# Strassen pairs in three of the down projection's four chunks, another cut of its last chunk, and regrouped recurrence matmuls

## The chip, the cores and the metric

One core of a Trainium2 chip runs the whole program. The metric is the device time of one execution in microseconds (us), the median of three. Lower is better.

## The reference, cut to what matters

One layer of a hybrid decoder for a prompt of 1024 rows and for 8 sample rows of one token each, width 1024. h2 has 1024 channels, the inner layer of the feed-forward part 4096.

```python
h = _rmsnorm(x, p['norm_mix']) * (1 + sc1) + sh1
proj = h @ p['w_in']
...
o_hg, S_new = _hgrn2_recurrence(qh, kh, vh, lh, S_hg.astype(f32))
...
y, h_new = _ssd_recurrence(...)
...
u = jax.nn.sigmoid(ga + bma) * (o_hg @ p['w_br_a']) + jax.nn.sigmoid(gb + bmb) * (y @ p['w_br_b'])
x = x + g1 * (u @ p['w_out'])

h2 = _rmsnorm(x, p['norm_mlp']) * (1 + sc2) + sh2
x = x + g2 * (jnp.square(jax.nn.relu(h2 @ p['w_up'])) @ p['w_down'])
...
y_prompt = _rmsnorm(xp, norm_final)
y_sample = _rmsnorm(xs, norm_final)
```

All of it is float32. The two recurrences run over the 1024 rows in chunks; the HGRN2 one has 8 heads, the SSM one 8 groups of 4 heads. The outputs are y, the new states of both recurrences and the last rows before the convolution.

## The kernel before

Activations lie with channels on the partitions: a *plane* is 128 channels by NT = 1032 columns (1024 prompt rows, 8 samples). Every float32 plane and weight is kept as two halves of the type that TensorE takes in one pass, hi (the value rounded) and lo (the rest), and a product is three matmuls: wh with lo, wl with hi, wh with hi.

A **dense block** makes one output plane from eight input planes: `load_w` (L47) brings a weight of 128 x 1024 by a DMA of SP into a staging tile "wr" (three buffers), ACT makes `wh` (L54), VectorE `wl` (L56), each with two buffers. `dense_split` (L79) runs over one of three column splits of SW = 344: 8 planes x 3 matmuls into a PSUM tile `acc` (three buffers), 72 for the whole block, and then an eviction. `tick` (L95) is called after every three matmuls: a recurrence can run beside the dense blocks as a generator, and each `yield n` lets n matmuls of dense blocks go by before it goes on. So the rows of HGRN heads (`hgrn_recurrence`, L460) and SSM groups (`ssm_recurrence`, L783) lie between the dense matmuls: in HGRN `kv_ps` (L529) and `o_ps` (L547), each in two half groups of four chunks, and the row sums of `row_rstd` (L559, matmul L564); in SSM, for each pair of heads, `kvx_ps` (L846), then `y_ps` (L881, from w and xdt, 64 output rows) and `yi_ps` (L885, from cv and hs), each in two halves.

A **Strassen pair** (`strassen_pair`, L1277) makes two output planes at once by seven products instead of eight, in the order 1, 7, 6, 2, 5, 4, 3; each product is two column quarters of HQ = 258 with 4 planes x 3 matmuls (L1304). Products 1, 2 and 3 take quarters of the planes as they are, 7, 6, 5 and 4 differences of them, the tiles `th` and `tl`. `differences` (L1104, lines L1108 on VectorE) makes four differences of 516 columns from two planes. `strassen_weights` (L1236) combines and splits the two weights (L1250).

`phase_ffn` (L1320) ends the kernel. The up projection is 2 + 4 dense blocks, 12 pairs and 2 dense blocks; its 32 output planes go to memory (`ad`, L1331). The down projection adds up four chunks of eight such planes, `down[c * 8 + m]` being the weight for output plane m. In chunks 0 to 2 each of eight dense blocks ends in `gated_add` (L1020, L1024, and L1027 and L1028 for the samples' 8 columns), which adds to x1. With block m goes `act` for plane m of the next chunk: `load_split_in` (L914) loads it by SP into the later `lo` (L920), ACT makes hi (L921) and VectorE lo (L922). Planes have two sets of buffers ("A1" and "Q3", "A0" and "Q2"), which chunks take in turn. The last chunk goes over the splits in the order LAST = (2, 0, 1); within one, over eight blocks, whose weights are loaded anew in each; after each block `sum_sq` (L1037, L1038) adds a square to `sqa`, and at the end `rstd_model` (L1041, matmul `ss` L1044, then the root, L169 to L174) and eight scalings (L1391) with eight DMAs of y (L1392).

A scheduler sets each engine's order from the order of the program and from priorities (`high_priority` for loads, splits and evictions); each engine, and SP's queue of loads, then goes in order.

## Time and profile before

| | us |
|---|---|
| three timed runs, median | 2486.53 (2486.45 to 2491.19) |
| the profiled execution | 2488.51 |
| its span | 2486.7 |
| TensorE busy | 2447.1 |
| VectorE busy | 1607.8 |
| ScalarE (ACT) busy | 1087.9 |
| dense 344-column matmuls on the chain, share | 58% |
| Strassen matmuls (L1304) on the chain, share | 13% |

The profile is that of one execution. The *chain* is the work that ended last, followed back from the last instruction. A row of a *group* gives line, engine, operation, tiles (out <- in), size and number, then busy time, mean ns of one, the idle time of the engine before them and what ended it. *Windows* give each engine's busy time in a stretch. A row of the *timeline* gives start, length, engine and what ran; the length of a matmul there is more than its share of TensorE, since matmuls overlap: what counts is the distance from one start to the next. *PEclk* is the granted clock of TensorE as a share of full speed.

### The profile page before, as it was taken

The numbers are of one execution on the slowest core, as the hardware profiler recorded it, in microseconds if no ns is written. First come the engines' busy times: TensorE is split into PE (matmuls) and PEld (weight loads), VectorE is DVE, ScalarE is ACT, GpSimd is POOL, SyncE is SP. The second block draws the span as 40 slices with busy tenths as digits, with TensorE's granted clock in tenths as the row PEclk, the third lists the DMA queues.
The fourth block names the chain that finished last, engine by engine and source line by source line (L and its number), as shares of the span: only waits on it lengthen the run. The fifth ranks groups of instructions, "written<-read, shape, count | busy, mean of one in ns | idle before, by whom it ended". The sixth has DMA issues, their size and how long they took to land.

```text
span 2486.7 us, 51048 instructions
## 1 busy us (share of the span) xinstructions
PE 2447.1 (98%) x21774; PEld 2388.0 (96%) x21774; DVE 1607.8 (65%) x2808; ACT 1087.9 (44%) x1730; POOL 112.3 (5%) x218
## 2 busy tenths in 40 slices
PE   8999999999999999999999999999999999999998
PEld 7999999999999999999998999999999999999997
DVE  7666665459798888876776634457975665443356
ACT  4444454466565556536555623124533334221133
POOL 0000000000000000000111000000012221000000
PEclk9999999999999999999999999999999999999999
DMA  6333333334445444533555744233233335233134
GB/s 260 121 113 122 105 123 113 118 102 154 151 144 175 130 165 146 182 115 109 178 188 179 248 135 146 76 112 133 97 108 102 107 103 203 95 113 107 55 107 148
DMA packets 110436, 335.07 MB, mean 135 GB/s; under 512 B 20000, under 2 KB 27024, under 8 KB 110192
## 3 DMA queue, kind: packets, MB, share of 16 engines
q1 hardware_dynamic: 93504, 278.93, 33.3%
q0 software_dynamic: 16272, 52.52, 6.1%
q8 instruction: 171, 2.80, 0.5%
q14 instruction: 57, 0.47, 0.1%
q10 hardware_dynamic: 432, 0.35, 0.0%
HBM read 262.16 MB, written 69.85 MB: 134 GB/s over the span
## 4 chain that ended last, share of the span: by engine, by line
PE 83%; issue 6%; DVE 5%; ACT 3%; DMA 2%; POOL 1%; DVEq 0%; POOLq 0%; ACTq 0%
PE acc L87 58%; PE b L1304 13%; PE lv_ps L584 2%; PE y_ps L881 1%; PE yi_ps L885 1%; PE kvx_ps L846 1%; PE acc L139 1%; PE o_ps L547 1%; POOL ad L1331 1%; DMA y<-yd 1%; PE ada_ps L203 1%; PE kv_ps L529 1%; DVE wl L1250 1%; PE cb_ps L808 1%; PE xt_ps L833 1%
## 5 line engine op out<-in xcount | busy, mean ns | idle before, releaser
L87 PE MATMUL acc<-hl,wh 128*128 128x344 f32 x1608 | 530.9, 330 | 1.0 <-issue 0.9
L87 PE MATMUL acc<-hh,wl 128*128 128x344 f32 x1608 | 515.6, 321 | 0.0
L87 PE MATMUL acc<-hh,wh 128*128 128x344 f32 x1608 | 514.6, 320 | 0.0
L87 PE MATMUL acc<-hi,wl 128*128 128x344 f32 x1248 | 400.4, 321 | 1.9 <-DVE wl L56 1.9
L87 PE MATMUL acc<-lo,wh 128*128 128x344 f32 x1248 | 398.8, 320 | 1.6 <-ACT wh L54 1.4
L87 PE MATMUL acc<-hi,wh 128*128 128x344 f32 x1248 | 399.3, 320 | 0.0
L54 ACT ACTIVATE wh<-wr 128x1024 fp32r<-128x1024 f32 x174 | 183.7, 1056 | 413.3 <-PE acc L87 310.7
L87 PEld LDWEIGHTS acc<-hl,wh 128*128 128x128 f32 x1608 | 302.4, 188 | 9.4 <-issue 7.0
L87 PEld LDWEIGHTS acc<-hh,wl 128*128 128x128 f32 x1608 | 302.7, 188 | 0.0
L87 PEld LDWEIGHTS acc<-hh,wh 128*128 128x128 f32 x1608 | 302.5, 188 | 0.0
L56 DVE TENSOR_TENSOR wl<-wr,wh 128x1024 fp32r<-128x1024 f32 x174 | 212.9, 1224 | 78.1 <-ACT wh L54 77.0
L87 PEld LDWEIGHTS acc<-hi,wl 128*128 128x128 f32 x1248 | 234.8, 188 | 2.7 <-DVE wl L56 2.5
L87 PEld LDWEIGHTS acc<-lo,wh 128*128 128x128 f32 x1248 | 234.8, 188 | 2.5 <-ACT wh L54 2.0
L87 PEld LDWEIGHTS acc<-hi,wh 128*128 128x128 f32 x1248 | 235.1, 188 | 0.2
L1304 PE MATMUL b<-th,wl 128*128 128x258 f32 x800 | 227.9, 285 | 6.2 <-DVE wl L1250 6.0
L1304 PE MATMUL b<-tl,wh 128*128 128x258 f32 x800 | 226.9, 284 | 0.0
L1304 PE MATMUL b<-th,wh 128*128 128x258 f32 x800 | 226.8, 284 | 0.0
L1024 DVE SCALAR_TENSOR_TENSOR x<-acc,modT,x 128x344 f32<-128x344 f32 (+1 forms) x120 | 68.7, 572 | 186.5 <-PE acc L87 186.1
L1304 PEld LDWEIGHTS b<-th,wl 128*128 128x128 f32 x800 | 152.0, 190 | 8.4 <-DVE wl L1250 8.2
L1304 PEld LDWEIGHTS b<-tl,wh 128*128 128x128 f32 x800 | 151.9, 190 | 4.5 <-issue 4.5
L1304 PEld LDWEIGHTS b<-th,wh 128*128 128x128 f32 x800 | 152.1, 190 | 0.0
L1250 DVE TENSOR_TENSOR wl<-wr,wh 128x512 fp32r<-128x512 f32 (+1 forms) x125 | 112.8, 902 | 58.4 <-ACT wh L1268 29.8
(313 smaller groups left out, 4738.3 us busy)
## 6 DMA issues: line engine op xcount, KB each, us to landing
wr<-w_ssm SPq DMA_DIRECT2D x48, 512.0 KB
wr<-w_down SPq DMA_DIRECT2D x48, 512.0 KB
wr<-w_ada SPq DMA_DIRECT2D x36, 512.0 KB
lo<-ad SPq DMA_DIRECT2D x32, 516.0 KB
wr<-w_hg SPq DMA_DIRECT2D x32, 512.0 KB
w<-cumd SPq DMA_DIRECT2D x32, 512.0 KB
wr<-w_up SPq DMA_DIRECT2D x32, 512.0 KB
ad<-r POOLq DMA_DIRECT2D x96, 129.0 KB, 2.1
```

The source lines that it names most:

```text
L54: nc.scalar.activation(wh, wr, AF.Copy)
L56: nc.vector.tensor_tensor(wl, wr, wh.bitcast(F32), op=ALU.subtract)
L87: last = nc.tensor.matmul(acc[:M, :SW], a[:, sl], b[:, cs(s)], start=(i == 0 and j == 0), stop=(i == n - 1 and j == 2))
L139: k.nc.tensor.matmul(ac[s][:, :SW], a[:, sl], b[:, cs(s)], start=(i == 0 and j == 0), stop=(i == self.n - 1 and j == 2))
L203: nc.tensor.matmul(ps[r, :64], k.scT[:, i, :], w[:, :, r], start=i == 0, stop=i == KD - 1, tile_position=(0, 32 * g))
L529: nc.tensor.matmul(ps[:, c * P:(c + 1) * P], ktok[:, cc], vtok[:, cc], start=True, stop=True)
L547: nc.tensor.matmul(ps[:, c * P:(c + 1) * P], a, x[:, c * P:(c + 1) * P], start=n == 0, stop=n == len(parts) - 1, skip_group_check=True)
L584: k.nc.tensor.matmul(out, QK[hf][:, HT + key:HT + key + 32], x, start=True, stop=True, tile_position=(0, 32 * g))
L808: nc.tensor.matmul(ps[:, c * P:(c + 1) * P], Bc[:, cc], Cc[:, cc], start=True, stop=True)
L1024: nc.vector.scalar_tensor_tensor(dst[:, :n], ps[:, :n], gate[:, 0:1], base[:, :n], ALU.mult, ALU.add)
L1250: nc.vector.tensor_tensor(out, x, y, op=ALU.subtract)
L1304: nc.tensor.matmul(acc, a[:, sl], x[:, cols], start=(p in (1, 7, 2) and i == 0 and j == 0), stop=(i == KD // 2 - 1 and j == 2), skip_group ...
```

## The change

- **Down chunks 0 to 2**: three dense blocks (m = 0 to 2), two Strassen pairs (m = 3, 4 and 5, 6), and a dense block m = 7, whose weight is split in two parts. During the three dense blocks `operands` is called four times: SP loads two of the chunk's planes a second time (516 KB each), VectorE makes four differences, ACT two `th` and VectorE two `tl`. They lie in the buffers of the plane set that the chunk itself does not use. The next chunk's eight planes are loaded into that same set, all eight `act` calls standing behind the pairs.
- **Pair evictions**: `add_pair` adds a kept product and the PSUM tile, and then calls `gated_add`.
- **Last chunk**: m = 0 to 2 are dense blocks of full width; the weights of m = 3 to 7 are loaded once and kept, two in the usual buffers and three in freed plane buffers; then come passes over 512, 264 and 256 columns, each with five blocks, sum, root, scalings and DMAs of y. The squares of m = 0 to 2 are summed beforehand.
- **HGRN**: all eight `kv_ps` matmuls stand in one group, both halves of `o_ps` in another; `row_rstd` is put off to the next head (at step h == 32).
- **SSM**: both halves of `kvx_ps` stand in one group, and both halves of `y_ps` ahead of the two `yi_ps`.

```diff
+COLS = (slice(520, NT), slice(256, 520), slice(0, 256))
...
-def load_w(k, src, prio=AHEAD):
+def load_w(k, src, prio=AHEAD, tiles=None, parts=1):
...
+        wh, wl = tiles or [k.wp.tile([P, KD * P], F32R, tag=t, name=t, bufs=2) for t in ("wh", "wl")]
+        for n in range(parts):
+            c = slice(n * KD * P // parts, (n + 1) * KD * P // parts)
+            nc.scalar.activation(wh[:, c], wr[:, c], AF.Copy)
+            nc.vector.tensor_tensor(wl[:, c], wr[:, c], wh[:, c].bitcast(F32), op=ALU.subtract)
...
@@ hgrn_head
+        elif h == 32:
+            for f in k.sums:
+                f()
+            k.sums.clear()
...
@@ hgrn_recurrence
+    kv = [rec_ps(k, "kv_ps") for _ in range(2)]
+    for ci in range(NCH):
+        cc = slice(ci * P, (ci + 1) * P)
+        nc.tensor.matmul(kv[ci // 4][:, ci % 4 * P:(ci % 4 + 1) * P], ktok[:, cc], vtok[:, cc], start=True, stop=True)
...
+    yield 27
...
-        yield 6
+    yield 9
...
-    yield 12
+    k.sums.append(lambda: row_rstd(k, sq, 1.0 / (P * P), k.rh[hd], [
+        k.sp.tile([P, SW], F32, tag=t, name=t, bufs=b) for t, b in (("nrm_a", 1), ("nrm_y", 2), ("nrm_t", 1))]))
...
@@ ssm_recurrence
+        kv = [rec_ps(k, "kvx_ps") for _ in range(2)]
+        for ci in range(NCH):
+            cc = slice(ci * P, (ci + 1) * P)
+            nc.tensor.matmul(kv[ci // 4][:, ci % 4 * P:(ci % 4 + 1) * P], btok[:, cc], xdec[:, cc], start=True, stop=True)
...
-            yield 12
+        yield 24
...
+        yp = [rec_ps(k, "y_ps") for _ in range(2)]
+        for ci in range(NCH):
+            cc = slice(ci % 4 * P, (ci % 4 + 1) * P)
+            for hh in range(2):
+                o1 = hh * 64
+                nc.tensor.matmul(yp[ci // 4][o1:o1 + 64, cc], xdt[:, ci * P + o1:ci * P + o1 + 64],
+                                 W[ci // 4][:, hh, cc], start=True, stop=True)
...
@@ phase_ffn
+    spare = []
+
+    def shape(c):
+        return 3, 2 if c < 3 else 0
+
+    def operands(c, T, i):
+        tags = "A%d" % (c % 2), "Q3" if c % 2 else "Q2"
+        if i == 0:
+            spare[:] = [[k.pp.tile([P, NT], F32, tag=t, name="ar") for t in tags] for _ in range(2)]
+        ps = [[k.pp.tile([P, NT], F32R, tag=t, name=n) for n in ("th", "tl")] for t in tags]
+        raw = spare[i % 2] if i < 3 else [stage(k) for _ in ps]
+        for n, r in enumerate(raw):
+            nc.sync.dma_start(r, ad[c * KD + i + 4 * n])
+        differences(k, *raw)
+        for (hi, lo), r, ts in zip(ps, raw, ((1, 3), (4, 2))):
+            nc.scalar.activation(hi, r, AF.Copy)
+            nc.vector.tensor_tensor(lo, r, hi.bitcast(F32), op=ALU.subtract)
+            for n, t in enumerate(ts):
+                T[t].append(tuple(y[:, n * HN:(n + 1) * HN] for y in (hi, lo)))
+    def add_pair(m0):
+        def evac(m, half, q, a, ps):
+            c = half * HN + q * HQ
+            c = slice(c, c + HQ)
+            if a is not None:
+                t = k.sp.tile([P, SW], F32, tag="sq", name="dt", bufs=2)[:, :HQ]
+                nc.vector.tensor_tensor(t, a, ps, op=ALU.add)
+                ps = t
+            x = x1[m0 + m][:, c]
+            gated_add(k, c, x, x, ps, k.modT[:, 40 + m0 + m, :])
+        return evac
...
+    for c in range(4):
+        T = {n: [] for n in (1, 2, 3, 4)}
+        ahead, pairs = shape(c)
+        for m in range(ahead):
+            for i in ((0, 1), (2,), (3,))[m] if pairs else ():
+                operands(c, T, i)
+            dense(k, down[c * KD + m], aX, add(m))
+        X = strassen_operands(aX, T) if pairs else None
+        for n in range(pairs):
+            m = ahead + 2 * n
+            strassen_pair(k, [down[c * KD + m + a] for a in range(2)], X, add_pair(m))
+        if c == 3:
+            break
+        nX = [act(c + 1, i) for i in range(KD)]
+        for m in range(ahead + 2 * pairs, KD):
+            dense(k, down[c * KD + m], aX, add(m), 2)
+        aX = nX
+    M0 = 3
+    free = [k.pp.tile([P, NT], F32R, tag=t, name="free") for t in ("A1", "Q3") for _ in range(8)]
+    ws = [load_w(k, down[3 * KD + m], tiles=None if m < M0 + 2 else [free[2 * (m - M0) - 4 + n][:, :KD * P] for n in range(2)])
+          for m in range(M0, KD)]
+    sq, sq2, sums, ra, rs = [t.bitcast(F32) for t in free[11:]]
+    for m in range(M0):
+        sum_sq(k, sums, x1[m], m == 0, (sq, sq2)[m % 2])
+    half = iter(range(1 << 20))
+    for c in COLS:
+        for m in range(M0, KD):
+            x = x1[m][:, c]
+            dense_split(k, ws[m - M0], aX, c, lambda s, ps: gated_add(k, s, x, x, ps, k.modT[:, 40 + m, :]))
+            o = next(half) % 2 * 512
+            sum_sq(k, sums[:, c], x, False, sq[:, o:o + c.stop - c.start])
+        y = rstd_model(k, sums[:, c], (ra[:, c], rs[:, c], sums[:, c]))
         for m in range(KD):
-            dense(k, down[c * KD + m], aX, add(m))
-            nX.append(act(c + 1, m))
-        aX = nX
-    for s in LAST:
-        acc = k.sp2.tile([P, SW], F32, tag="sqa", name="sqa", bufs=1)
-        for m in range(KD):
-            w = load_w(k, down[3 * KD + m])
-            dense_split(k, w, aX, s, add(m))
-            sum_sq(k, acc, x1[m][:, cs(s)], m == 0)
-        y = rstd_model(k, acc)
-        for m in range(KD):
-            xx = x1[m][:, cs(s)]
-            nc.vector.scalar_tensor_tensor(xx, xx, k.norm_final[:, m:m + 1], y, ALU.mult, ALU.mult)
-            nc.sync.dma_start(k.o["y"][m][:, cs(s)], xx)
+            x = x1[m][:, c]
+            nc.vector.scalar_tensor_tensor(x, x, k.norm_final[:, m:m + 1], y, ALU.mult, ALU.mult)
+            nc.sync.dma_start(k.o["y"][m][:, c], x)
```

Three places in the engines' order follow. The first is TensorE at the start of the second chunk's first block (before, the start of chunk 1); lo and hi are the chunk's planes, wh and wl the weight. Before:

```order
L87 MATMUL acc_24563<-lo_23909,wh_24559 128x344
L87 MATMUL acc_24563<-hi_23908,wl_24561 128x344
L87 MATMUL acc_24563<-hi_23908,wh_24559 128x344
L87 MATMUL acc_24563<-lo_24001,wh_24559 128x344
L87 MATMUL acc_24563<-hi_24000,wl_24561 128x344
L87 MATMUL acc_24563<-hi_24000,wh_24559 128x344
L87 MATMUL acc_24563<-lo_24093,wh_24559 128x344
L87 MATMUL acc_24563<-hi_24092,wl_24561 128x344
L87 MATMUL acc_24563<-hi_24092,wh_24559 128x344
L87 MATMUL acc_24563<-lo_24185,wh_24559 128x344
L87 MATMUL acc_24563<-hi_24184,wl_24561 128x344
L87 MATMUL acc_24563<-hi_24184,wh_24559 128x344
```

After, from the block's seventh matmul on, where lo_24621, lo_24626, lo_24631 and lo_24636 are planes 0 to 3:

```order
L90 MATMUL acc_24787<-lo_24631,wh_24783 128x344
L90 MATMUL acc_24787<-hi_24630,wl_24784 128x344
L90 MATMUL acc_24787<-hi_24630,wh_24783 128x344
L90 MATMUL acc_24813<-lo_24621,wh_24783 128x344
L90 MATMUL acc_24813<-hi_24620,wl_24784 128x344
L90 MATMUL acc_24813<-hi_24620,wh_24783 128x344
L90 MATMUL acc_24813<-lo_24626,wh_24783 128x344
L90 MATMUL acc_24787<-lo_24636,wh_24783 128x344
L90 MATMUL acc_24787<-hi_24635,wl_24784 128x344
L90 MATMUL acc_24787<-hi_24635,wh_24783 128x344
```

Before, a split goes through its planes in order of number; after, the second split's first four matmuls, on planes 0 and 1, are put ahead of the first split's matmuls on plane 3, which is the last one loaded: 13 matmuls stand ahead of them. At the start of the last chunk it is 27, nine of each of the three splits.

The second is VectorE from the last eviction of chunk 2 on; x1_18917 is output plane 7, x1_18903 output plane 0, wl the low half of a weight. Before:

```order
L1024 SCALAR_TENSOR_TENSOR x1_18917<-acc_25995,modT_145,x1_18917 128x336
L1027 TENSOR_TENSOR ga_26021<-acc_25995,modT_145 128x8
L1028 TENSOR_TENSOR x1_18917<-ga_26021,x1_18917 128x8
L56 TENSOR_TENSOR wl_26070<-wr_26066,wh_26068 128x1024
L1024 SCALAR_TENSOR_TENSOR x1_18903<-acc_26036,modT_145,x1_18903 128x336
L1027 TENSOR_TENSOR ga_26062<-acc_26036,modT_145 128x8
```

After, where lo_26512 and lo_26492 are planes 31 and 27 of the last chunk:

```order
L1031 SCALAR_TENSOR_TENSOR x1_18917<-acc_26576,modT_145,x1_18917 128x336
L1034 TENSOR_TENSOR ga_26602<-acc_26576,modT_145 128x8
L927 TENSOR_TENSOR lo_26512<-lo_26512,hi_26511 128x1032
L1035 TENSOR_TENSOR x1_18917<-ga_26602,x1_18917 128x8
L58 TENSOR_TENSOR wl_26695<-wr_26692,wh_26694 128x1024
L927 TENSOR_TENSOR lo_26492<-lo_26492,hi_26491 128x1032
L1031 SCALAR_TENSOR_TENSOR x1_18903<-acc_26611,modT_145,x1_18903 128x344
```

Two plane splits have moved behind the last eviction of the chunk, with a weight split between them, ahead of the next block's first eviction.

The third is TensorE in the first SSM group, around the second half of y and yi of one pair of heads; the acc rows are a dense block's. Before:

```order
L87 MATMUL acc<-hh,wl 128x344
L87 MATMUL acc<-hh,wh 128x344
L881 MATMUL y_ps<-w,xdt 64x128 x8
L885 MATMUL yi_ps<-cv,hs 128x128 x4
L87 MATMUL acc<-hl,wh 128x344
L87 MATMUL acc<-hh,wl 128x344
```

After, with the second y group moved up to the first (there y_ps x16 now, followed by yi_ps x3):

```order
L90 MATMUL acc<-hh,wl 128x344
L90 MATMUL acc<-hh,wh 128x344
L890 MATMUL yi_ps<-cv,hs 128x128 x4
L90 MATMUL acc<-hl,wh 128x344
L90 MATMUL acc<-hh,wl 128x344
L90 MATMUL acc<-hh,wh 128x344
```

The second yi group stands alone between dense matmuls. Of 32 y groups 23 are left; kvx groups go from 32 to 28, kv and o groups from 16 to 8 each. The row sums of HGRN (`ss`, x3) stay eight groups between dense matmuls.

More of the change, by code (lines that the diff above doesn't have):

```diff
@@ L81, in dense_split @@
     nc = k.nc
-    acc = k.ps.tile([P, 512], F32, tag="acc", name="acc", bufs=3)
+    c = cs(s) if isinstance(s, int) else s
+    acc = k.ps.tile([P, 512], F32, tag="acc", name="acc", bufs=3)[:M, :c.stop - c.start]
     n = len(X)
@@ L86, in dense_split @@
         for j, (a, b) in enumerate(((wh, xl), (wl, xh), (wh, xh))):
-            last = nc.tensor.matmul(acc[:M, :SW], a[:, sl], b[:, cs(s)],
-                                    start=(i == 0 and j == 0), stop=(i == n - 1 and j == 2))
+            last = nc.tensor.matmul(acc, a[:, sl], b[:, c], start=(i == 0 and j == 0), stop=(i == n - 1 and j == 2))
         tick(k, 3)
     with k.tc.high_priority(AHEAD):
-        evac(s, acc[:M, :SW])
+        evac(s, acc)
     return last
@@ L641, in phase_hgrn @@
     k.side, k.left = None, 0
+    k.sums = []
     for hd in range(H):
@@ L841, in ssm_recurrence @@
         hs = plane("hs")
+        kv = [rec_ps(k, "kvx_ps") for _ in range(2)]
+        for ci in range(NCH):
+            cc = slice(ci * P, (ci + 1) * P)
+            nc.tensor.matmul(kv[ci // 4][:, ci % 4 * P:(ci % 4 + 1) * P], btok[:, cc], xdec[:, cc], start=True, stop=True)
         for hf in range(2):
-            ps = rec_ps(k, "kvx_ps")
-            for c in range(4):
-                cc = slice((hf * 4 + c) * P, (hf * 4 + c + 1) * P)
-                nc.tensor.matmul(ps[:, c * P:(c + 1) * P], btok[:, cc], xdec[:, cc], start=True, stop=True)
+            ps = kv[hf]
             for c in range(4):
@@ L871, in ssm_recurrence @@
         yield 15
+        yp = [rec_ps(k, "y_ps") for _ in range(2)]
+        for ci in range(NCH):
+            cc = slice(ci % 4 * P, (ci % 4 + 1) * P)
[3 more added lines that the diff above has]
+                                 W[ci // 4][:, hh, cc], start=True, stop=True)
         for hf in range(2):
             sl = slice(hf * 512, (hf + 1) * 512)
-            ps, pi = rec_ps(k, "y_ps"), rec_ps(k, "yi_ps")
+            ps, pi = yp[hf], rec_ps(k, "yi_ps")
             c0 = 1 - hf
-            for c in range(4):
-                ci = hf * 4 + c
-                cc = slice(c * P, (c + 1) * P)
-                for hh in range(2):
-                    o1 = hh * 64
-                    nc.tensor.matmul(ps[o1:o1 + 64, cc], xdt[:, ci * P + o1:ci * P + o1 + 64],
-                                     W[hf][:, hh, cc], start=True, stop=True)
             for c in range(c0, 4):
@@ L1028, in gated_add, with sum_sq @@
         nc.vector.tensor_tensor(dst[:, n:], t, base[:, n:], op=ALU.add)
-def sum_sq(k, acc, x, first):
+def sum_sq(k, acc, x, first, t=None):
     nc = k.nc
@@ L1035, in sum_sq, with rstd_model @@
         return
-    t = k.sp.tile([P, SW], F32, tag="sq", name="sq", bufs=2)
+    if t is None:
+        t = k.sp.tile([P, SW], F32, tag="sq", name="sq", bufs=2)
     nc.scalar.activation(t, x, AF.Square)
     nc.vector.tensor_tensor(acc, acc, t, op=ALU.add)
-def rstd_model(k, acc):
+def rstd_model(k, acc, tiles=None):
     nc = k.nc
+    n = acc.shape[1]
     ps = rec_ps(k, "ss")
-    nc.tensor.matmul(ps[:, :SW], k.ones, acc, start=True, stop=True)
-    return rstd_from(k, ps[:, :SW], SW, 1.0 / 1024)
+    nc.tensor.matmul(ps[:, :n], k.ones, acc, start=True, stop=True)
+    return rstd_from(k, ps[:, :n], n, 1.0 / 1024, tiles)
 def phase_out(k, uX):
@@ L1274, in strassen_weights, with strassen_pair @@
     return W
-def strassen_pair(k, srcs, X, evac):
+def strassen_pair(k, srcs, X, evac, last=3):
     nc = k.nc
@@ L1294, in keep @@
         snap[p, q] = t
-    for p, b in ((1, 1), (7, 2), (6, 1), (2, 3), (5, 1), (4, 2), (3, 1)):
+    for p in (1, 7, 6, 2, 5, 4, 3) if last == 3 else (1, 7, 6, 5, 4, 3, 2):
+        b = {7: 2, 4: 2, 2: 3}.get(p, 1)
         for q in range(2):
@@ L1442, in body @@
                 finish(k)
+                k.sums.pop()()
                 dt_phase(k)
```

37 lines of the change are left out of this document (11 added, 26 removed).

## The prediction

> **What bounds the kernel now.** I began with the page: the span, the engines' shares and the chain of work that ended last.
>
> ```profile
> span 2486.7 us, 51048 instructions
> PE 2447.1 (98%) x21774; PEld 2388.0 (96%) x21774; DVE 1607.8 (65%) x2808; ACT 1087.9 (44%) x1730; POOL 112.3 (5%) x218
> PE 83%; issue 6%; DVE 5%; ACT 3%; DMA 2%; POOL 1%; DVEq 0%; POOLq 0%; ACTq 0%
> ```
>
> TensorE is busy for 98% of the span and carries 83% of the chain: a saving must shorten its stream or one of the few stretches in which it stands. The profiled run took 2488.51 us, 1.81 more than its span and 1.98 more than the median of the three runs, 2486.53; I work out a difference and take it off both.
>
> What a matmul costs at either width comes from the windows view, one stretch of Strassen products alone and one of dense blocks alone; each row gives the length and then each engine's busy time with its number of instructions. Two rows of the whole chain (start, length, matmuls) stand beside it: a shorter Strassen stretch, and the end of the kernel.
>
> ```profile
> core 0: us, PE busy (x) PEld busy (x) DVE busy (x) ACT busy (x) POOL busy (x), PEclk, DMA share, GB/s
> 1940.00:2080.00 140.00, 140.00 (x1171) 140.00 (x1171) 87.72 (x160) 48.26 (x91) 30.09 (x56) 1.00 0.31 106
> 2120.00:2380.00 260.00, 260.00 (x1654) 260.00 (x1653) 95.18 (x159) 43.83 (x42) 0.00 (x0) 1.00 0.25 84
> ```
>
> ```profile
> 1134.76 20.45 PE b L1304 x168
> 2086.74 327.79 PE acc L87 x2083
> ```
>
> A 258-column product matmul takes 140/1171 = 119.6 ns (121.7 in the chain's row), a 344-column dense one 260/1654 = 157.2 ns. The last row says that from 2086.74 to 2414.53 nothing but dense matmuls is on the chain: before the change no plane, weight or eviction stops TensorE in the down phase. VectorE works 95 of 260 us there, so there is room, but only if it lies where it is needed.
>
> **Strassen pairs (+).** A pair is 168 matmuls instead of 2 x 72 = 144: 168 x 0.1196 = 20.09 against 144 x 0.1572 = 22.64, 2.55 us less. Six pairs: -15.3; at 121.7 ns 2.19 each, -13.1, which is the bound. The pair breaks even at 22.64/168 = 134.8 ns. [...]
>
> **Operands, in a chunk's first three blocks.** Each chunk makes 16 differences on VectorE (128x516) and eight splits of two instructions, ACT's and VectorE's (128x1032), from eight loads of SP. These are rows of the same forms in the up phase and in the down phase.
>
> ```profile
> L1108 DVE TENSOR_TENSOR wr<-wr x16: 689/695/697, 1788.6 to 1825.4; 128x516 f32<-128x516 f32 x16
> L922 DVE TENSOR_TENSOR lo<-lo,hi 128x1032 fp32r<-128x1032 f32 x32 | 38.8, 1230 | 15.0 <-ACT hi L921 14.8
> L921 ACT ACTIVATE hi<-lo 128x1032 fp32r<-128x1032 f32 x32 | 34.0, 1065 | 42.8 <-DMA lo<-ad 42.8
> L1024 DVE SCALAR_TENSOR_TENSOR x<-acc,modT,x 128x344 f32<-128x344 f32 x64 | 36.8, 575 | 101.2 <-PE acc L87 101.0
> L56 DVE TENSOR_TENSOR wl<-wr,wh 128x1024 fp32r<-128x1024 f32 x50 | 61.2, 1224 | 12.8 <-ACT wh L54 12.8
> L1250 DVE TENSOR_TENSOR wr<-wr 128x512 f32<-128x512 f32 x75 | 51.8, 691 | 1.9
> ```
>
> VectorE's bill for them is 16 x 0.695 + 8 x 1.23 = 21.0 us. Beside it stand nine evictions (9 x 0.575 = 5.2), two weight splits (2.4) and the first combinations of the pair's weights (some 3 of 0.69): 30.6. TensorE has 3 x 72 x 0.1572 = 34.0 us of these blocks, and 24 x 0.1196 = 2.9 more of product 1, which takes plain quarters; only product 7 needs a difference. So 36.8 against 30.6: some 6 us of slack, and I take **0**. Without that cover each microsecond beyond it counts, in each of three chunks (a rival below). Within the pairs: an up pair of the windows' first row keeps VectorE 87.72/6.97 = 12.6 of its 20.1 us, and a down pair evicts in as many instructions (14): 0 as well. SP's extra loads stand in its queue behind the planes and ahead of weights that are wanted a block later; ACT's eight extra splits (8.5 us) go into an engine that works 44 of 260 us.
>
> **Planes at the three chunk boundaries.** The operands lie in the buffers into which before loaded the next chunk's planes a whole chunk early. Now these loads wait in SP's queue until products 5 and 4 of the second pair have read them, and behind them wait the weights of later blocks; block m=0 of the next chunk waits for the planes. How fast planes come is in SP's and ACT's timeline near the end of chunk 0 (start, length, issues; ACT's rows are the hi halves).
>
> ```profile
> 2196.50 3.67 SPq L920 DMA_DIRECT2D lo<-ad  x5
> 2200.02 1.07 ACT L921 ACTIVATE hi<-lo 128x1032 fp32r<-128x1032 f32 x1 [10.17 <-DMA lo<-ad]
> ...
> 2202.45 1.07 ACT L921 ACTIVATE hi<-lo 128x1032 fp32r<-128x1032 f32 x1 [0.41 <-DMA lo<-ad]
> ...
> 2206.46 1.07 ACT L921 ACTIVATE hi<-lo 128x1032 fp32r<-128x1032 f32 x1 [0.25 <-DMA lo<-ad]
> ```
>
> The first plane is there 3.5 us after its issue, each further one (2206.46 - 2202.45)/3 = 1.33 later. I count from the end of block m=7. It takes 72 x 0.1572 = 11.3, product 3 before it 2.9; so the first load can start at -14.2, lands at -10.7, and the eighth at -10.7 + 7 x 1.33 = -1.4. Its hi ends at -0.3; VectorE then has the last eviction (0.57), a small one (0.16) and the lo half (1.23): ready at 2.0. In the order block m=0 of chunks 1 and 2 has 13 matmuls before it needs that plane, 13 x 0.157 = 2.04: nothing to spare, and nothing lost. At the boundary to chunk 3 two weights go ahead of the last three planes (2 x 1.33, taken as planes): the last lands at 1.3. VectorE has the eviction, 0.16, one lo, one wl and the last lo after the block's end, 0.57 + 0.16 + 1.23 + 1.22 + 1.23 = 4.4 with some 0.1 between; the order has 27 matmuls = 4.24 before it. Sum **+0.8** for the three; between 0 and +4 (one plane's 1.33 late at each).
>
> **Last chunk.** Three blocks are dense at full width; five go in passes of 512, 264 and 256 columns, 1032 as before, in as many matmuls: 0 for TensorE. Their weights are loaded once, not thrice. What the narrower last pass shortens is the tail, from the chain of waits of the last 22 us, VectorE's and SP's timelines there, and rows of one operation at two widths from about 2000 to 2110:
>
> ```profile
> 2464.85 8.68 PE acc L87 x55
> ...
> 2475.32 0.86 PE ss L1044 x2
> ...
> 2476.20 0.56 ACT nrm_a L169
> ...
> 2480.54 2.92 DVE x L1391 x6
> ```
>
> ```profile
> 2479.48 3.99 DVE L1391 SCALAR_TENSOR_TENSOR x<-x,cst,nrm_y 128x344 f32<-128x344 f32 x8
> ```
>
> ```profile
> 2480.08 3.76 SPq L1392 DMA_DIRECT2D out_y<-x  x8
> ```
>
> ```profile
> L1335 DVE TENSOR_TENSOR r<-r 128x258 f32<-128x258 f32 x10 | 4.2, 422 | 0.9 <-ACT r L1334 0.9
> L1335 DVE TENSOR_TENSOR r<-r 128x344 f32<-128x344 f32 x5 | 2.6, 514 | 0.1
> L1334 ACT ACTIVATE r<-b 128x258 f32<-128x258 f32 x10 | 3.9, 386 | 3.5 <-PE b L1304 3.2 <-DMA ad<-r 0.2
> L1334 ACT ACTIVATE r<-acc 128x344 f32<-128x344 f32 x5 | 2.2, 446 | 1.3 <-PE acc L87 1.3
> ```
>
> After the last dense matmul come one by one 13 instructions of VectorE (one eviction, one sum, three of the root, eight scalings), four of ACT and the sum on TensorE. 86 columns less save VectorE 92 ns and ACT 60 each, the sum 0.86 x 88/344 = 0.22: 13 x 0.092 + 4 x 0.060 + 0.22 = 1.7. The last scalings may be paced by SP's issues (3.76/8 = 0.47 each) and not by VectorE (0.50); then seven of them give 0.03 and not 0.09, and 1.2 is left. I take **-1.4**, between -0.9 and -1.7.
>
> **Recurrences beside the dense blocks.** Matmuls of other shapes break the dense stream. The rows are PE's timeline in an SSM group, and the whole kernel's row for y_ps with min, median and max.
>
> ```profile
> 568.49 1.09 PE L881 MATMUL y_ps<-w,xdt 128*64 128x128 f32 x16
> 569.51 0.94 PE L885 MATMUL yi_ps<-cv,hs 128*128 128x128 f32 x6
> 570.21 0.41 PE L87 MATMUL acc<-hl,wh 128*128 128x344 f32 x1
> ...
> 572.03 0.31 PE L87 MATMUL acc<-hh,wh 128*128 128x344 f32 x1
> 572.27 1.09 PE L881 MATMUL y_ps<-w,xdt 128*64 128x128 f32 x16
> 573.29 1.16 PE L885 MATMUL yi_ps<-cv,hs 128*128 128x128 f32 x8
> 574.21 0.40 PE L87 MATMUL acc<-hl,wh 128*128 128x344 f32 x1
> ```
>
> ```profile
> 560.77 1.05 PE L846 MATMUL kvx_ps<-xdec,btok 128*128 128x128 f32 x8
> 561.58 0.41 PE L87 MATMUL acc<-hh,wh 128*128 128x344 f32 x1
> ```
>
> ```profile
> L881 PE MATMUL y_ps<-w,xdt x512: 272/273/324, 568.5 to 1061.0; 128*64 128x128 f32 x171
> ```
>
> The second half costs 574.21 - 572.03 = 2.18 us, 2.02 above a dense matmul's 0.157. Sixteen y records are (1.09 - 0.27)/15 = 55 ns apart, yet yi begins 1.02 after the first: the turn from y to yi costs. Joined, the second y costs 16 x 0.055 = 0.88 and its yi, alone like kvx, about 0.81: 1.69, or 0.33 less. In the order 9 of the 32 y groups are joined to another (32 become 23 groups); the other 7 halves get a dense run between their y groups, a turn fewer and a break more, taken as 0. 9 x 0.33: **-3.0**, between -0.3 (0.19 for each of nine, by 1.02/16 a record, and 0.2 lost in seven) and -5.3 (all sixteen). Kv and o go from 16 to 8 groups each, kvx from 32 to 28. A break costs 572.27 - 572.03 - 0.157 = 0.08, so 20 breaks less are worth 1.6 at most; but the 0.81 of a kvx group is its eight records' own pitch, which a joined group keeps, so I take 0. The row sums leave their place but come between dense matmuls again: 0.
>
> **Sum.** -15.3 + 0.8 - 1.4 - 3.0 = -18.9: the profiled run 2469.6, the median **2467.6 us**. With all terms at their ends 2462.6 to 2476.2.
>
> **Rivals.**
> *The planes come late* (slower). If the loads start only when block m=7 ends (a buffer read longer than I think, or a queue entry ahead that waits), the last plane is ready 3.5 + 7 x 1.33 + 1.07 + 1.23 = 15.1 us after; less the 2.0, 2.0 and 4.2 of matmuls that go first, TensorE stands 13.1, 13.1 and 10.9 = 37.1. A stand also costs clock, as the windows view shows around one of 3.59 us:
>
> ```profile
> 1346.90:1350.40 3.50, 0.00 (x0) 0.00 (x1) 1.85 (x3) 0.48 (x1) 0.00 (x0) 1.00 0.26 107
> 1350.60:1353.90 3.30, 3.30 (x17) 3.30 (x17) 3.27 (x4) 2.45 (x5) 0.53 (x1) 0.50 0.41 118
> ```
>
> Seventeen matmuls in 3.30 us at clock 0.50, 194 ns each against 120, lose some 1.3 us; three times 3.9. Then 37.1 + 3.9 - 19.7 (the rest of the sum) = +21.3: 2507.8 us. It is slower than before from (19.7 + 5)/3 = 8.2 us a boundary, that is loads that start within 5 us of the block's end. Against it: the second pair's last reader is product 4, 14 us ahead. Chance 0.06. Its milder form, loads from the pair's end on (-11.3): 1.8 + 1.8, 2471.2; 0.08. In between, near no change: 0.06.
> *VectorE becomes the bound in the first three blocks.* In-order waits (a difference behind a load, an eviction behind a block) eat the 6 us and 4 more in each chunk: +12, 2479.6. For it: 30.6 of 36.8 us is close. 0.09.
> *The regroupings give nothing*, because each new break takes what a joined one gave: 2470.6. 0.13.
> *They give more*, each break being worth more than I priced: below 2463.5. 0.05.
> *Width hardly counts.* [...] Both stretches of rows speak against it: 0.01.
>
> **How the numbers follow.** The forecast has 0.52. Faster: 0.52 + 0.08 + 0.09 + 0.13 + 0.05 = 0.87; within 0.2% (5 us, about what a measurement of this kernel can tell from no change) 0.06 + 0.01 = 0.07; slower 0.06. The range, 2463.5 to 2480.0, holds forecast, mild planes, the regroupings' loss and most of VectorE's case: 0.52 + 0.08 + 0.13 + 0.07 = 0.80.
>
> **What would show it.** Right: product matmuls of the down phase near 120 ns; no stand over 0.5 us of TensorE at a chunk's first block or before product 7 of its first pair; 11.6 us from the last dense matmul's end to the span's (13.2 - 1.4 or so); fewer y groups, each half group 0.3 shorter. Wrong: PE idle with ACT hi or DVE lo as releaser at a boundary (the planes); PE idle before product 7 with DVE as releaser (VectorE); a clock of 0.50 in either place.

## The result, and the profile after

| | before | after |
|---|---|---|
| median of six runs, us | 2486.49 (2485.02 to 2491.19) | 2470.27 (2465.89 to 2473.25) |
| ratio, 95% interval | | 0.9929 (0.9916 to 0.9942) |
| profiled run, us | 2488.51 | 2468.79 |
| its span, us | 2486.7 | 2466.9 |

The changed kernel is faster by 16.2 us between the medians, by 14.4 to 20.9 by the interval; 18.9 were forecast. The page of the changed kernel:

```profile
span 2466.9 us, 51549 instructions
PE 2429.1 (98%) x21918; PEld 2365.5 (96%) x21918; DVE 1685.2 (68%) x2953; ACT 1118.9 (45%) x1789; POOL 112.7 (5%) x218
PE 84%; DVE 5%; DMA 4%; ACT 3%; issue 3%; POOL 0%; DVEq 0%; ACTq 0%; POOLq 0%
```

TensorE has 144 records more and is 18 us less busy, at 98% as before. What each engine added (VectorE 77 us, ACT 31) did not become the bound.

Where the time went shows when the span is cut where the program's stages meet. These are differences between starts of TensorE's records (the last dense matmul by its end), in us, for two profiles of each kernel:

| stretch | before | before, again | after | after, again |
|---|---|---|---|---|
| start to the first `cb_ps` (HGRN) | 547.98 | 547.28 | 548.00 | 549.13 |
| first `cb_ps` to the gates' first product (SSM) | 560.56 | 560.49 | 558.75 | 559.22 |
| gates: thirteen Strassen pairs | 282.96 | 283.45 | 279.52 | 282.62 |
| merge, to the first up pair | 451.75 | 449.11 | 451.68 | 453.00 |
| the up pairs | 243.32 | 242.34 | 242.98 | 242.11 |
| end of up and down, to the last dense matmul | 386.94 | 386.96 | 373.94 | 374.04 |
| tail, from there to the end | 13.18 | 13.27 | 12.04 | 12.09 |

Three rows move in both pairs by more than one kernel differs from itself: down by -13.0, the tail by -1.1 to -1.2, SSM by -1.3 to -1.8, together 15.4 to 16.0. The rest goes up and down by some microseconds in either kernel; 3.4 us of the 19.8 between the first two spans lie in the gates, which the change does not touch.

### The profile page after: what moved, and what is told of

Read it like the earlier page. It is cut to its first block, busy times and chain, and to the rows that moved or that the text cites. A ratio compares the mean times of both kernels' runs of the same rounds, so it can differ in the third digit from the quotient of the medians.

```text
span 2466.9 us, 51549 instructions
## 1 busy us (share of the span) xinstructions
PE 2429.1 (98%) x21918; PEld 2365.5 (96%) x21918; DVE 1685.2 (68%) x2953; ACT 1118.9 (45%) x1789; POOL 112.7 (5%) x218
## 4 chain that ended last, share of the span: by engine, by line
PE 84%; DVE 5%; DMA 4%; ACT 3%; issue 3%; POOL 0%; DVEq 0%; ACTq 0%; POOLq 0%
PE acc L90 55%; PE b L1314 17%; PE lv_ps L587 2%; PE y_ps L882 1%; PE kvx_ps L849 1%; PE o_ps L551 1%; PE yi_ps L890 1%; PE acc L141 1%; DMA y<-yd 1%; DMA wr<-od 1%; DVE wl L58 1%; PE ada_ps L205 1%; PE kv_ps L534 1%; DVE wl L1259 1%; PE cb_ps L812 1%
## 5 line engine op out<-in xcount | busy, mean ns | idle before, releaser
L90 PE MATMUL acc<-hi,wl 128*128 128x344 f32 (+3 forms) x888 | 285.2, 321 | 1.9 <-DVE wl L58 1.8
L1314 PE MATMUL b<-th,wl 128*128 128x258 f32 x992 | 281.4, 284 | 5.6 <-DVE wl L1259 5.4
L90 PE MATMUL acc<-lo,wh 128*128 128x344 f32 (+3 forms) x888 | 283.8, 321 | 1.4 <-ACT wh L57 1.4
L90 PE MATMUL acc<-hi,wh 128*128 128x344 f32 (+3 forms) x888 | 284.2, 320 | 0.0
L57 ACT ACTIVATE wh<-wr 128x1024 fp32r<-128x1024 f32 (+1 forms) x146 | 151.0, 1037 | 218.9 <-PE acc L90 148.3
L58 DVE TENSOR_TENSOR wl<-wr,wh 128x1024 fp32r<-128x1024 f32 (+1 forms) x146 | 175.2, 1201 | 69.2 <-ACT wh L57 68.2
L90 PEld LDWEIGHTS acc<-hi,wl 128*128 128x128 f32 x888 | 167.3, 188 | 4.3 <-DVE wl L58 3.3
L90 PEld LDWEIGHTS acc<-lo,wh 128*128 128x128 f32 x888 | 167.0, 189 | 3.4 <-ACT wh L57 2.0
L90 PEld LDWEIGHTS acc<-hi,wh 128*128 128x128 f32 x888 | 167.5, 189 | 0.7
L756 DVE SCALAR_TENSOR_TENSOR cv<-raw,cst,cv 128x1024 f32<-128x1024 f32 x96 | 122.5, 1276 | 0.5
```

Source lines behind the costliest of these rows:

```text
L57: nc.scalar.activation(wh[:, c], wr[:, c], AF.Copy)
L58: nc.vector.tensor_tensor(wl[:, c], wr[:, c], wh[:, c].bitcast(F32), op=ALU.subtract)
L90: last = nc.tensor.matmul(acc, a[:, sl], b[:, c], start=(i == 0 and j == 0), stop=(i == n - 1 and j == 2))
L756: nc.vector.scalar_tensor_tensor(cv[:, :T], raw[:, j:j + T], cw[:, j:j + 1], cv[:, :T], ALU.mult, ALU.add)
L1314: nc.tensor.matmul(acc, a[:, sl], x[:, cols], start=(p in (1, 7, 2) and i == 0 and j == 0), stop=(i == KD // 2 - 1 and j == 2), skip_group ...
```

## Experiments

All twelve run beside the kernel before. The same stretches, in us, from each one's profile, and its ratio to the kernel before with the interval:

| run | HGRN | SSM | gates | down | tail | ratio |
|---|---|---|---|---|---|---|
| e1_pairs | 549.50 | 560.80 | 279.22 | 374.95 | 13.29 | 0.9955 (0.9942 to 0.9967) |
| e2_ssm | 547.88 | 559.16 | 282.21 | 386.97 | 13.20 | 0.9984 (0.9974 to 0.9995) |
| e3_hgrn | 547.41 | 560.90 | 279.92 | 386.78 | 13.18 | 0.9986 (0.9977 to 0.9995) |
| e4_last | 551.16 | 560.64 | 285.08 | 387.35 | 12.10 | 1.0001 (0.9992 to 1.0010) |
| e5_weight_first | 547.64 | 558.80 | 280.22 | 375.97 | 12.12 | 0.9912 (0.9895 to 0.9928) |
| e6_no_cover | 547.71 | 559.36 | 279.54 | 408.17 | 12.06 | 1.0053 (1.0035 to 1.0072) |
| e7_more_vector | 547.76 | 558.52 | 280.87 | 379.84 | 12.04 | 0.9938 (0.9920 to 0.9957) |
| e8_two_ahead | 548.30 | 558.50 | 279.49 | 381.66 | 12.05 | 0.9941 (0.9920 to 0.9961) |
| e9_last128 | 549.31 | 559.30 | 280.79 | 381.84 | 10.39 | 0.9951 (0.9936 to 0.9966) |
| e10_y_only | 547.88 | 558.38 | 278.79 | 374.10 | 12.09 | 0.9930 (0.9913 to 0.9946) |

### The change in four parts

**e1_pairs**: the kernel before with the pairs of the down phase, without the rest.

```diff
     for c in range(3):
-        nX = []
-        for m in range(KD):
+        T = {n: [] for n in (1, 2, 3, 4)}
+        ahead, pairs = shape(c)
+        for m in range(ahead):
...
     for s in LAST:
```

> The kernel before with only the six Strassen pairs of the down phase (operands, pair evictions, planes loaded behind the pairs, block m=7); the last chunk and the recurrences as before. Theory (the pairs save 2.55 us each and little of it is lost): 14 to 15.3 us faster than before, 2471 to 2473, and the same small stands of TensorE at block m=7 and at the chunk boundaries as in the whole change, 1 to 2 us together. Rival (the pairs save less and the rest of the change carries the gain): under 10 us faster.

Down is 374.95 against 386.94 to 386.96: -12.0, and 11.2 us (8.2 to 14.4) by the ratio. The theory's mechanism holds, its size does not quite: one stand, a split into the last chunk, took 1.7 us (from 2364.99 to 2366.82, less a pitch), where the changed kernel has none of that size. TensorE waits there for VectorE's low half of the second block's weight, which the old last chunk wants after one split (24 matmuls) and the new one after three.

**e2_ssm**, **e3_hgrn** and **e4_last**: the kernel before with one other part each.

```diff
+        yp = [rec_ps(k, "y_ps") for _ in range(2)]
```

```diff
+    kv = [rec_ps(k, "kv_ps") for _ in range(2)]
...
+    k.sums.append(lambda: row_rstd(k, sq, 1.0 / (P * P), k.rh[hd], [
```

```diff
+    for m in range(3):
+        dense(k, down[3 * KD + m], aX, add(m))
+    M0 = 3
```

> The kernel before with only the SSM regrouping (kvx in one group, both y groups ahead of yi). By the two traces, from the first cb_ps matmul to the first product of the gates the changed kernel is 1.8 us shorter. Theory (the regrouping gives this): 1.8 us faster than before in that stretch, and nothing elsewhere that is its own. Rival (the prediction's price): 3.0. Second rival (the stretch moved by chance): 0.

SSM takes 559.16 against 560.5 to 560.9 in every kernel with the old order: -1.3 to -1.7, the theory's size; the ratio's 4.0 us (1.2 to 6.5) holds it and 3.0 as well.

> The kernel before with only the HGRN regrouping (kv in one group, o in another, row sums put off to the next head). Theory (a break saved is a break moved): the time to the first cb_ps matmul stays within 0.3 us of 548.0, and the whole within what runs differ by. Rival (16 breaks less at 0.08): 1.3 us shorter.

Its stretch is 547.41, against 547.28 and 547.98: nothing that can be told from no change there. The ratio says 3.5 us faster (1.2 to 5.7), and the profile puts no such gain in HGRN: its run is short in the gates (279.92), where its code is the same and kernels with the old HGRN gave 279.22 and 285.08. With the old HGRN put back beside everything else (e10) the ratio is 0.9930 against 0.9929. So the theory stands by the stretch, and what the ratio shows stays open.

> The kernel before with only the last chunk's change (three full blocks, five weights kept, passes of 512, 264 and 256 columns). Theory (only the tail gets shorter): 1.2 to 1.4 us faster, from the last dense matmul's end to the span's 12.0 and not 13.2 us, and the dense matmuls take as long as before. Rival (passes of unequal width cost TensorE something): the last chunk's matmuls together over 0.4 us longer, and the gain is gone.

The tail is 12.10 (-1.1), down 387.35 (+0.4): -0.7 in all, which the ratio cannot tell from nothing. Both the theory and its rival had a part: the tail came, and TensorE lost 0.4 around the sums between the passes (1.9 us at the two against 1.5 before). By their stretches the four parts add up to 14.0 us (11.9, 1.4, 0 and 0.7), some 1.5 short of the whole; the stand in e1, which only the old last chunk has, is of that size.

### The stands in the down phase

In the changed kernel TensorE stands not so much where I looked, at the chunk's boundary, as eleven microseconds ahead of it, at the third record of block m=7, the first that reads the weight's low half. PE's timeline there in chunk 1, and VectorE's:

```profile
2263.90 0.48 PE L90 MATMUL acc<-lo,wh 128*128 128x344 f32 x2
2264.69 0.42 PE L90 MATMUL acc<-hi,wl 128*128 128x344 f32 x1 [0.31 <-DVE wl L58]
```

```profile
2262.01 1.23 DVE L927 TENSOR_TENSOR lo<-lo,hi 128x1032 fp32r<-128x1032 f32 x1 [0.36 <-ACT hi L926]
2263.16 0.48 DVE L1031 SCALAR_TENSOR_TENSOR x<-dt,modT,x 128x258 f32<-128x258 f32 x1
2263.56 0.48 DVE L1031 SCALAR_TENSOR_TENSOR x<-b,modT,x 128x258 f32<-128x258 f32 x1
2263.96 0.68 DVE L58 TENSOR_TENSOR wl<-wr,wh 128x512 fp32r<-128x512 f32 x1
```

The low half of the first plane of the next chunk and two evictions go ahead of the low half of the weight that TensorE wants at 2264.21, two pitches after 2263.90. Over the pitch of 157 ns these stands are 0.34, 0.58 and 0.30 us, 1.2 in the three chunks; the boundaries themselves lose 0.4.

**e5_weight_first** lets ACT and VectorE split that weight ahead of the planes.

```diff
+        w7 = load_w(k, down[c * KD + 7], parts=2)
+        nX = [act(c + 1, i, (k.wh_last, k.wl_last)) for i in range(KD)]
```

> The changed kernel, but ACT and VectorE split block m=7's weight ahead of the next chunk's planes. In the changed kernel TensorE stands 0.2 to 0.6 us at the second matmul of that block in each chunk, where VectorE's low half of the weight comes behind a plane's low half (1.23 us) and evictions. Theory (that order is the cause of these stands): they go, 1.0 to 1.4 us less in all than the changed kernel, and the chunk boundaries stay within 0.3 us of theirs. Rival (the weight's buffer, freed only by product 4, is the cause): the stands stay. Second rival (the planes, put back, are now late at the boundary): the gain returns there.

The stands at block m=7 are gone, so their order was the cause. But the second rival holds: the planes are late by what they were put back, as the waits of PE in the down phase show (engine, line, releaser, total us, times, longest), where the changed kernel has no such row:

```profile
PE acc L90 <- DVE lo L927: 2.6, 4, 1.2
```

Down is 375.97, 2.0 longer than in the changed kernel. The ratio, 0.9912 (0.9895 to 0.9928), does not tell the two apart. In this order the cost moves and grows; whether a third order would save it, no run shows.

**e6_no_cover** puts four dense blocks ahead of the pairs and none behind.

```diff
-        return 3, 2 if c < 3 else 0
+        return (4, 2) if c < 3 else (3, 0)
```

> The changed kernel with four dense blocks ahead of the two pairs and none behind, in chunks 0 to 2: as many matmuls, but no block m=7 to cover the planes' loads. Theory (that block is the cover, as the prediction worked out): loads start at the end of product 4, 2.9 us ahead of the chunk's end; the last plane is ready 12 us behind it, and TensorE stands some 10 us at each of three boundaries, with a clock of 0.50 after it: 30 to 43 us over the changed kernel, slower than before by 14 to 27. Rival (planes land early whatever stands behind the pairs): no more than 3 us over the changed kernel.

Down is 34.2 us longer than in the changed kernel, and the kernel slower than before by 0.53% (0.35 to 0.72), 13 us. The 34.2 lie within the 30 to 43 expected, the 13 just under the 14 to 27. The late planes of the prediction's first rival are real, though made here by another order of blocks than the rival had. PE's waits in the down phase, and windows around the boundary to chunk 1 (length, PE busy and records, granted clock, share of the DMA engines, GB/s):

```profile
PE acc L90 <- DVE lo L927: 20.7, 9, 3.6
PE acc L90 <- DVE wl L58: 1.6, 3, 0.6
```

```profile
2190.50:2193.60 3.10, 0.25 (x2) 1.00 1.00 405
2195.40:2197.40 2.00, 0.51 (x2) 0.50 1.02 420
2202.50:2207.90 5.40, 5.31 (x18) 0.50 0.23 60
```

The planes and the loads between them come at 405 to 420 GB/s with all DMA engines busy, and each of ACT's hi halves there waits for its plane's transfer, 1.28 us after the one before: it is the transfers that TensorE waits for, and after the stands it runs on at half clock (0.50) for 5.4 us more. One dense block behind the pairs is worth all of this.

**e7_more_vector** and **e8_two_ahead** ask how much room VectorE has ahead of product 7.

```diff
+        for _ in range(6):
+            t = k.sp2.tile([P, SW], F32, tag="mt", name="xx", bufs=2)
+            nc.vector.tensor_tensor(t, x1[0][:, :SW], x1[0][:, :SW], op=ALU.mult)
```

```diff
-        return 3, 2 if c < 3 else 0
+        return (2, 2) if c < 3 else (3, 0)
...
-            for i in ((0, 1), (2,), (3,))[m] if pairs else ():
+            for i in ((0, 1), (2, 3))[m] if pairs else ():
```

> The changed kernel with 24 more VectorE instructions of 128x344 in each of chunks 0 to 2, six beside each call that makes operands: 12.3 us of added work whose results nobody reads. Theory (VectorE has some 6 us of slack ahead of product 7 in chunks 1 and 2, and 10 in chunk 0): TensorE stands before product 7 of the first pair by 6 us in chunks 1 and 2 and 2 in chunk 0, 12 to 15 us over the changed kernel. Rival (VectorE is far from binding there): under 2 us. Second rival (no slack at all): 35.

Down is 5.9 us longer, between the theory and the first rival. The scheduler did not keep the added instructions in their chunks: 36 ran in chunk 0, 24 in chunk 1, 12 in chunk 2, and some behind product 7. In chunk 1 seventeen of them, 8.7 us, came ahead of product 7's weight on a VectorE without a break, and TensorE stood for 1.9 us: some 7 us of room, by which the prediction's 6 was near. (In chunk 2, with twelve, VectorE itself waited 1.5 us for that weight's transfer, so the stand there says less.)

> The changed kernel with two dense blocks ahead of the pairs and two behind, in chunks 0 to 2. Theory (the first blocks are VectorE's time for operands, the block behind the pairs is the planes' time): 11.3 us less for VectorE, of which its slack and the moved block's own evictions cover some 8 to 9: stands of 2 to 4 us before product 7 in chunks 1 and 2, 4 to 8 us over the changed kernel, and none at the boundaries. Rival (the place of the pairs does not matter): as the changed kernel within 1 us.

Down is 7.7 us longer, within the 4 to 8 expected, but it is not spread as expected: the first pairs of chunks 0, 1 and 2 take 4.8, 2.7 and 1.0 us over the pitch, where chunk 0 was to have none and chunk 2 as much as chunk 1. (Of the 4.8 some 1.5 are half clock behind a stand of 2.6.) In chunk 1 product 7 waits for its weight, and VectorE, which combines it, for the weight's transfer:

```profile
2218.72 0.51 PE L1314 MATMUL b<-tl,wh 128*128 128x258 f32 x2 [1.76 <-ACT wh L1269]
2219.45 0.39 PE L1314 MATMUL b<-th,wl 128*128 128x258 f32 x1 [0.22 <-DVE wl L1259]
```

```profile
2213.23 1.23 DVE L1402 TENSOR_TENSOR tl<-wr,th 128x1032 fp32r<-128x1032 f32 x1
2217.31 0.69 DVE L1259 TENSOR_TENSOR wr<-wr 128x512 f32<-128x512 f32 x1 [2.09 <-DMA wr<-w_down]
```

SP issues that load at 2214.49, as soon as the last low half of an operand (2213.23 + 1.23) has read its staging tile, and VectorE then idles for 2.09 us. So what the operands delay is the weight's load, and these stands hold a transfer; they do not measure VectorE's room by itself.

The gain at the boundary from a second covering block is 0.2 us a chunk or less. Three blocks ahead and one behind are thus a balance: one block less on either side costs 8 or 34 us.

### Widths

**e9_last128** narrows the last pass to 128 columns.

```diff
-COLS = (slice(520, NT), slice(256, 520), slice(0, 256))
+COLS = (slice(520, NT), slice(128, 520), slice(0, 128))
```

> The changed kernel with passes of 512, 392 and 128 columns in its last chunk. Theory (the matmul pitch falls with width on the straight line through 119.6 ns at 258 and 157.2 at 344, and the tail's instructions shorten by about 1.07 ns a column, the scalings as far as SP's issues let them): the last chunk's matmuls take as long as in the changed kernel, and the tail from the last dense matmul's end falls from 12.0 to about 10.5 us: 1.5 us less in all. Rival (a floor near 105 ns under narrow matmuls, as the recurrences' 128-column records show): 120 matmuls 37 ns longer, 4.4 us more, and a loss of some 3 us.

The tail is 10.39, 1.65 less, as the theory has it; but down is 7.9 longer, and the kernel is 0.2% behind the changed one by the ratios, whose intervals overlap a little. The rival holds in kind and was priced too low: a triple of matmuls takes 232 + 179 + 112 = 523 ns and not 471, 6.2 us for the 120, and the rest of the 7.9 comes from longer waits, at the second sum between the passes (1.1) and at the start of the last chunk (1.0), less 0.4 in other places. A row of windows in the last pass of this kernel, and one in the 512-column pass of the changed kernel:

```profile
2454.00:2465.00 11.00, 11.00 (x101) 1.00 0.41 148
```

```profile
2399.00:2423.00 24.00, 24.00 (x105) 1.00 0.00 1
```

From start to start the medians are 112 ns at 128 columns, 118 at 256, 121 at 264, 157 at 344, 179 at 392 and 232 at 512. From 264 on each column costs 0.45 ns; below, hardly anything more is saved (0.05 ns a column from 256 down to 128). The Strassen products' 258 columns, at 120 ns, lie close to that bend. What sets the floor, no run here shows.

### The recurrences, and what runs differ by

**e10_y_only** takes kvx, kv, o and the row sums back and keeps the y groups.

```diff
-        kv = [rec_ps(k, "kvx_ps") for _ in range(2)]
...
         for hf in range(2):
-            ps = kv[hf]
+            ps = rec_ps(k, "kvx_ps")
```

> The changed kernel with kvx, kv and o in two half groups each again and the row sums in their old place; the y groups stay regrouped. By the two traces the y groups gave 3.55 us, and the joined kvx groups cost 1.7 of them. Theory (a joined group of full 128 x 128 matmuls costs more than two single ones: 1.70 against twice 0.81, and it waits for the whole of its input): 557.1 us from the first cb_ps matmul to the first product of the gates, 1.7 less than the changed kernel; the groups of kv and o together 1.4 us less, the time to the first cb_ps matmul within what two runs of one kernel differ by. Rival (the losses lie in the y groups): 558.7 there.

Its SSM stretch is 558.38, between theory and rival and nearer the rival; two profiles of the changed kernel differ by 0.5 there. What a group costs is the time from the dense matmul ahead of it to the one behind, less a pitch of 157 ns. Summed over the SSM stretch:

| group, us | before | after | e10_y_only |
|---|---|---|---|
| y and yi | 61.30 | 57.75 | 57.74 |
| kvx | 25.90 | 27.58 | 26.88 |

The y groups gave 3.55 us, kvx took 1.7 of them back, and putting kvx back returned only 0.7: the other 1.0 stay where only the y groups are changed, as waits of four single kvx groups. PE's timeline shows the two ways in which kvx lost, a joined group and one that waits:

```profile
643.81 1.95 PE L849 MATMUL kvx_ps<-xdec,btok 128*128 128x128 f32 x16
645.51 0.40 PE L90 MATMUL acc<-hl,wh 128*128 128x344 f32 x1
...
584.84 1.13 PE L849 MATMUL kvx_ps<-xdec,btok 128*128 128x128 f32 x8 [0.27 <-DVE xdec L839]
```

The joined group costs 1.70 (645.51 - 643.81), two single ones 2 x 0.81 = 1.62, so the four joined ones lose 0.3. The four waits take 1.4 us in the changed kernel. In HGRN the kv groups, with the od matmuls in some of them, and the o groups cost 43.3 us joined and 41.9 apart: there too a break saved is nothing saved, though the stretch does not show the 1.4.

**e11_before_again** and **e12_after_again** are the two kernels once more, for a second profile.

> The kernel before once more, for a second profile of it. Theory (the gates phase, whose code the change does not touch, waits for transfers whose time differs from run to run): the stretch from the gates' first product to the next dense block differs from 282.96 us by a microsecond or more, and the down phase from 386.94 by less than 0.3. Rival (that stretch is a property of the kernel): 282.7 to 283.2 again.

> The changed kernel once more, for a second profile of it. Theory (as for the kernel before): the gates' stretch differs from 279.52 us by half a microsecond or more, the SSM stretch repeats 558.75 and the down phase 373.94 within 0.5. Rival (the change shortened the gates' stretch by 3.4 us): 279.3 to 279.7 again.

The gates of the kernel before repeat within 0.5 us, less than expected; those of the changed kernel give 282.62 after 279.52, against the rival. Down repeats within 0.1 us in both, SSM within 0.5. What moves the gates are TensorE's waits for a weight's low half and slow stretches of its clock. The waits there, in the order of the table's columns:

```profile
PE b L1304 <- DVE wl L1250: 8.1, 6, 3.6
PE b L1304 <- DVE wl L1250: 8.6, 6, 2.8
PE b L1314 <- DVE wl L1259: 6.0, 5, 2.1
PE b L1314 <- DVE wl L1259: 6.2, 5, 2.6
```

The clock is halved for one stretch of 3.4 us in each of the first two, for none in the third and for two in the fourth. At 1.4 us each (worked out in the last section), 273.5, 273.5, 273.5 and 273.6 us are left: the 3.1 us between the two profiles of the changed kernel are its two slow stretches. Behind some of the waits lie transfers whose time differs from run to run. Two profiles of the kernel before, the same instruction ahead of a weight's low half in VectorE's order:

```profile
1348.51 1.23 DVE L1167 TENSOR_TENSOR y<-y,z 128x1032 f32<-128x1032 f32 x1 [3.83 <-DMA y<-yd]
```

```profile
1348.23 1.23 DVE L1167 TENSOR_TENSOR y<-y,z 128x1032 f32<-128x1032 f32 x1 [2.19 <-DMA y<-yd]
```

Elsewhere in the same two profiles it is the other way round (1.68 and 3.09 us near 1217), so the sums come out close. Whether the change shortens the gates' waits on the average stays open: the stretch takes 278.8 to 282.6 us in the eight profiles that have the pairs and the new y groups, 279.2 to 285.1 in the six others.

## Why the prediction held, point by point

- **Pairs, -15.3.** The 1008 product matmuls of the down phase take 40.26 + 40.28 + 40.31 = 120.85 us, where 864 dense ones would take 135.82: **-15.0**. Rows of windows of the changed kernel: 39.00 us for 327 product records, 119.3 ns, and 30.00 for 192 dense ones, 156.3. The pitch of the up phase could be carried over. The rival that width hardly counts was priced with a pitch that no run shows; here 258 columns, 0.75 of 344, took 0.76 of the time (119.3/156.3).

```profile
2138.00:2177.00 39.00, 39.00 (x327) 1.00 0.26 85
2106.00:2136.00 30.00, 30.00 (x192) 1.00 0.43 148
```

- **Operands, 0.** Right: no stand ahead of product 7 in the changed kernel. e7 shows some 7 us of room in chunk 1, so VectorE's bill of 30.6 in 36.8 us was sound there, and its rival stayed away by that much.
- **Planes at the boundaries, +0.8.** Mechanism right, size short: **+1.6**, 0.4 at the boundaries and 1.2 at block m=7. The step that failed is "VectorE then has the last eviction (0.57), a small one (0.16) and the lo half (1.23)": it follows VectorE's queue from the end of block m=7 on and not from its start, where the first planes' halves stand ahead of that block's own weight. In e5 the cost moved to the boundaries and was not saved. Planes that come late cost 34 us (e6); block m=7 keeps that off.
- **Last chunk, 0 for TensorE.** Right for the passes: 232 + 121 + 118 = 471 ns a triple of matmuls, three times 157. What else the down phase lost is **+0.35** in the changed kernel and 0.4 in e4, most of it at the two sums between the passes.
- **Tail, -1.4.** It measured **-1.1 to -1.2**. The chain of waits at the end of the changed kernel, where 256 columns now run:

```profile
2454.90 0.50 DVE x L1031
...
2456.41 0.71 PE ss L1053 x2
...
2457.14 0.48 ACT free L171
...
2459.92 0.48 DVE x L1452
...
2460.80 2.38 DVE x L1452 x6
```

The eviction went from 0.59 to 0.50, the sum from 0.86 to 0.71, ACT's first from 0.56 to 0.48, six scalings from 2.92 to 2.38, and the chain from the last matmul to the last scaling's end is 1.6 us shorter, as the first sum had it (1.7). But from that end to the span's it is 3.72 us (2466.9 - 2463.18) where it was 3.24 (2486.7 - 2483.46). SP's queue shows why:

```profile
2460.44 3.76 SPq L1453 DMA_DIRECT2D out_y<-x  x8
```

The eight issues take 3.76 us, as long as before, while the scalings now come every 0.40 (2.38/6): the last issue starts 0.6 us behind the last scaling's end, where before it followed at once. That is the prediction's "paced by SP's issues", with 1.2; the step that failed is to take -1.4, between that and the full sum. (The 11.6 us that it then named as a sign should have been 13.2 - 1.4 = 11.8; it is 12.0.)

- **Recurrences, -3.0.** **-1.3 to -1.8**. Its y term was near, 3.55 for 3.0, with the joined group as worked out: 2.67 us (568.51 to 571.10, and its break) against 1.80 + 0.88. The term that failed is kvx, "its eight records' own pitch, which a joined group keeps, so I take 0": kvx cost 1.7, 0.3 of it because a joined group takes 1.70 and not 1.62, the rest in waits for its input, of which the prediction has none. With kvx apart again (e10) 1.0 of it stayed.

```profile
568.51 1.97 PE L882 MATMUL y_ps<-w,xdt 128*64 128x128 f32 x32
570.41 0.94 PE L890 MATMUL yi_ps<-cv,hs 128*128 128x128 f32 x6
571.10 0.41 PE L90 MATMUL acc<-hl,wh 128*128 128x344 f32 x1
```

With these terms, -15.0 + 1.6 + 0.35 - 1.15 - 1.55 = -15.75: the sum of the three stretches that moved, and near the -16.2 of the medians. The forecast was 3 us too good, most of it in two costs that I took at nothing: the stands at block m=7 and kvx. The median, 2470.3, lies as it happens on the prediction's rival of regroupings that give nothing (2470.6). The stretches tell the two apart in part: the SSM regrouping gave 1.3 to 1.8 us, and the HGRN one nothing that shows.

## What to carry to other kernels

Trade matmul columns only down to the width where the pitch stops falling: here 258 columns cost 120 ns, 128 still 112, and a pass that is narrower than that loses more than its shorter tail gives (in e9, 7.9 us against 1.65). When a buffer is turned over to new use, ask which block of work stands between its last reader and the first need of its next content, and follow the splitting engine's queue from the first of those loads, not from the last. At a kernel's end, price the queue that issues the stores beside the engine that makes them: here it kept its 0.47 us an issue when the scalings fell to 0.40. Join groups of matmuls only after pricing a group by itself from the trace: two kvx groups cost 1.62 us apart and 1.70 joined.
